# Keys and values of a bidirectional mLSTM and attention block as one product of quarters in seven products

## The chip, the cores and the metric

The kernel runs on one core of a Trainium2 chip. The metric is the device time of one execution in microseconds (us); 1239.61 us is the median of three runs of the kernel before (1238.98 to 1239.66). A core has a matrix engine (PE, which multiplies a stationary 128x128 tile by a moving tile of up to 512 columns into PSUM), a vector engine (DVE), an activation engine (ACT), GpSimd (POOL), and queues that issue transfers (DMAs): those of SP, ACT and POOL here.

## The reference

One layer over 1024 tokens of width 1024. Everything below is fp32 in the reference; the kernel splits each factor of a product into a high and a low part and takes three matmuls for each product.

```python
def rms(x, g):
    xf = x.astype(jnp.float32)
    return xf * lax.rsqrt(jnp.mean(xf * xf, axis=-1, keepdims=True) + EPS) * g.astype(jnp.float32)

# per layer:  p = rms(x, g1) @ w_in, its columns cut into
#   mLSTM:     q|k 0:1024 (behind a 5-wide convolution and silu), v 1024:1536, o 1536:2048, gates 2048:2064
#   attention: q 2064:2576, k 2576:3088, v 3088:3600
# x = x + concat(mlstm, attention) @ w_out ;  x = x + relu(rms(x, g2) @ w_1)**2 @ w_2

def diff_attention_group(qa, ka, va, q_g, k_g, ...):
    q = rms(q, q_g) * (HD_A ** -0.5)          # over 64 values of a head
    k = rms(k, k_g)
    logits = jnp.einsum('bmhqd,bmhkd->bmhqk', qblk, k) + bias
```

Two of these column blocks matter here: the attention keys (512 columns, called keys below) and the mLSTM values (512 columns, called values). The norm of a row of x, a factor `rcol` for each token, can be taken before or behind the product, since it scales rows.

## The kernel before

The activations stand transposed: `hhi[k]` and `hlo[k]` (k = 0 to 7, 128 channels by 1024 tokens) are the high and low part of x times the gain g1, not yet scaled by `rcol`. A weight tile is loaded raw, its high part made on ACT or DVE, and its low part by a subtraction on DVE or POOL.

The opening runs in this order on PE. [...] The values come first (L239): for each of 8 channel blocks, 8 token blocks and 3 matmuls, 192 matmuls of 512 columns into eight PSUM banks, as `x` arrives by SP. Then keys and gates together (`pkg`, L138 to L140 in the helper `mm3`): 8 token blocks with 48 matmuls each, of 256 or 272 columns. Then the queries (`pqa`): 192 matmuls of 512. Then the projections `pj_c` of the mLSTM queries and keys, in columns c4, c0 and so on, 48 matmuls of 512 each. From c0 on, a table of times places work between matmuls (six matmuls to a tick).

Beside the products, `head_norm` (L339 to L349) makes the norm of a token block's heads: a scaled copy from PSUM on ACT, a square on ACT, a sum and an addition on DVE, a power on POOL (L89), and a multiplication on DVE that is put off to the next block (`norm_end`). `gt` (L436) takes the gates out of the same PSUM tile. `head_turn` (L357) transposes normed heads on PE (tiles `pz`, two PSUM buffers of the tag sA) and splits the result on ACT and DVE into `zz`, which ACT's queue stores. `gates()` (from `pgt`, L446) turns the gates into decays: a chain of small steps over PE, DVE, ACT and POOL with tiles `pe`, `pm`, `pt`, also of sA. It runs during the queries. `distance_bias` fills a table of 2048 distances by 32 small DVE operations. POOL loads the row-wise x (`xr`, L251) for `rcol`.

Of the kernel before, what the change touches and what calls it, by code (L numbers as in the profile page):

```python
# [10 lines left out]
F32 = mybir.dt.float32  # L11
# [5 lines left out]
P = 128  # L17
S = 1024
# [29 lines left out]

@with_exitstack
def hybrid_block_kernel(ctx: ExitStack, tc: tile.TileContext, xT, xR, w_v, w_kg, w_c, w_va, w_qa, w_o, w_1, w_2, vec, rel, outT):  # L50
# [139 lines left out]
    stp = sctx.enter_context(tc.tile_pool(reuse_waits="tile", name="start", bufs=2, side="right"))  # L190
    with tc.tile_pool(reuse_waits="tile", name="ps0", bufs=8, space=PSUM) as ps0:
        lam = stp.tile([P, 256], F32, name="lam", bufs=1)
        total = stp.tile([P, NC], F32, name="total", bufs=1)
        rpad = stp.tile([P, 32], F32, name="rpad", bufs=1)
        rrow = stp.tile([P, 32], F32, name="rrow", bufs=1)
        pv = [ps0.tile([P, HB], F32, tag="pv", name=f"pv{t}") for t in range(NC)]

        for _ in range(9):
            nc.tensor.matmul(pv[0][:, 0:P], ones, ones, start=True, stop=True)
        xts = {}  # L200
        for k in range(KT):

            parts = 2 if k < 2 else 1
            n = S // parts
            xts[k] = xt = stp.tile([P, S], F32, tag="xt", name=f"xt{k}", bufs=4)
            if k == 0:

                whi, wlo, raw_v = w_tiles("v0")
                nc.scalar.dma_start(raw_v[:, 0:HB], w_v[0][:, 0:HB])

                nc.scalar.activation(mhalf, ones[:, 0:16], AF.Copy, scale=-0.5)
                nc.vector.tensor_copy(whi[:, 0:HB], raw_v[:, 0:HB])
            elif k % 2 == 0:
                whi, wlo, wload = wstage(f"v{k}", nc.vector)
                wload(w_v[k // 2], 0, 1024)
            for i in range(parts):
                sl = slice(i * n, (i + 1) * n)
                if k == 0 and i == 0:
                    nc.sync.dma_start(vecs[:, 0:V_CW], vec[:, 0:V_CW])
                load = nc.sync.dma_start(xt[:, sl], xT[k][:, sl])  # L220
                nc.scalar.activation(hhi[k][:, sl], xt[:, sl], AF.Copy, scale=vcol(V_G1 + k))
                last = nc.vector.scalar_tensor_tensor(
                    hlo[k][:, sl], xt[:, sl], vcol(V_G1 + k), hhi[k][:, sl].bitcast(F32), op0=ALU.mult, op1=ALU.subtract
                )
                if k == 0:

                    h = slice(i * HB, (i + 1) * HB)
                    if i == 1:
                        nc.sync.dma_start(raw_v[:, h], w_v[0][:, h])
                        nc.scalar.activation(whi[:, h], raw_v[:, h], AF.Copy)  # L230
                    nc.vector.tensor_tensor(wlo[:, h], raw_v[:, h], whi[:, h].bitcast(F32), op=ALU.subtract)
            o = (k % 2) * HB
            ops = [(hhi[k], whi), (hlo[k], whi), (hhi[k], wlo)]
            order = [(t, i) for t in range(NC) for i in range(3)]
            if k == 0:
                order = [(t, i) for h in range(2) for i in range(3) for t in range(4 * h, 4 * h + 4)]
            for t, i in order:
                a, b = ops[i]
                nc.tensor.matmul(  # L239
                    pv[t], a[:, t * P : (t + 1) * P], b[:, o : o + HB], start=k == 0 and i == 0, stop=k == KT - 1 and i == 2  # L240
                )
            if k == 2:
                with tc.issue_after(load.ins):
                    nc.sync.dma_start(vecs[:, V_CW:], vec[:, V_CW:V_LM])
                    nc.sync.dma_start(lam, vec[:, V_LM:])
            if k == 5:
                with tc.issue_after(last.ins):
                    parameters()
        for t in range(NC):
            xr = stp.tile([P, S], F32, tag="xt", name=f"xr{t}", bufs=4)  # L250
            nc.gpsimd.dma_start(xr, xR[t])  # L251
            nc.scalar.activation(xr, xr, AF.Square, accum_out=total[:, t : t + 1])
        nc.vector.tensor_scalar(rcol, total, 1.0 / D, EPS, op0=ALU.mult, op1=ALU.add)
        rsqrt(rcol, rcol, NC)
        nc.gpsimd.memset(rpad, 0.0)
        nc.vector.tensor_copy(rpad[:, 0:NC], rcol)
        nc.vector.transpose(rrow, rpad)
        for g in range(4):
            nc.gpsimd.dma_start(r_dram[:, 32 * g : 32 * g + 32], rrow[32 * g : 32 * g + NC, :])
        nc.gpsimd.dma_start(rb, bass.AP(tensor=r_dram.tensor, offset=r_dram.offset, ap=[[0, P], [1, S]]))  # L260
        vr = [stp.tile([P, S], F32, tag="xt", name=f"vr{i}", bufs=4) for i in range(4)]
        vr = [vr[t // 2][:, (t % 2) * HB : (t % 2 + 1) * HB] for t in range(NC)]
        for t in range(NC):
            if t % 2 == 0:
                nc.scalar.activation(vr[t], pv[t], AF.Copy, scale=rcol[:, t : t + 1])
            else:
                nc.vector.tensor_scalar(vr[t], pv[t], rcol[:, t : t + 1], None, op0=ALU.mult)
            nc.scalar.dma_start(vm_dram[t], vr[t])
# [67 lines left out]
    def head_norm(pool, src, z, t, name):  # L336

        zt = z
        nc.scalar.activation(zt.rearrange("p (a b) -> p a b", a=src.shape[1]), src, AF.Copy, scale=rcol[:, t : t + 1])  # L339
        sq = pool.tile([P, 8, 64], F32, tag="zsq", name=f"zsq{name}{t}", bufs=2)  # L340
        nc.scalar.activation(sq.rearrange("p a b -> p (a b)"), zt, AF.Square)
        ss = pool.tile([P, 8], F32, tag="zss", name=f"zss{name}{t}", bufs=2)
        nc.vector.tensor_reduce(ss, sq, axis=mybir.AxisListType.X, op=ALU.add)
        last = nc.vector.tensor_scalar(ss, ss, 64 * EPS, None, op0=ALU.add)
# [4 lines left out]
        ends.append(lambda: nc.vector.tensor_tensor(z8, z8, ss[:, :, None].to_broadcast([P, 8, 64]), op=ALU.mult))  # L349

# [6 lines left out]
    def head_turn(pool, tag, bufs, z, g, is_q):  # L357
# [7 lines left out]
        for h in range(NH):  # L365
# [16 lines left out]
            nc.scalar.dma_start(dst[h][g], zz.bitcast(F32))  # L382
# [4 lines left out]
    def distance_bias():  # L387

        rt = kgp.tile([NH, 32], F32, name="rt")
        nc.sync.dma_start(rt, rel.rearrange("b h -> h b"))  # L390
        bt = kgp.tile([NH, 2048], F32, name="bt")
        nc.vector.memset(bt[:, 2047:2048], 0.0)
        for b, first, end in _buckets():
            nc.vector.tensor_scalar(
                bt[:, first:end], rt[:, b : b + 1].to_broadcast([NH, end - first]), -1.0, None, op0=ALU.mult
            )
        nc.scalar.dma_start(bt_dram, bt)

    def key_weights(i):

        w = w_tiles(f"kg{i}", 1088)
        raw = w[2][:, 0 : 2 * N_HALF].rearrange("p (i n) -> p i n", i=2)
        hi, lo = (x.rearrange("p (i n) -> p i n", i=2)[:, :, 544 - N_HALF :] for x in w[:2])
        nc.sync.dma_start(raw, w_kg[i].rearrange("p (i n) -> p i n", i=2))
        nc.scalar.activation(hi, raw, AF.Copy)
        nc.vector.tensor_tensor(lo, raw, hi.bitcast(F32), op=ALU.subtract)
        return hi, lo

    wkg = [key_weights(i) for i in range(4)]
    halves = (slice(0, 256), slice(256, N_HALF))  # L410
    gt = gp.tile([P, 2, 8, NC], F32, name="gt")
    z1 = gp.tile([P, 4, HB], F32, name="z1")
    zs = [kgp.tile([P, 4, HB], F32, tag="z", name=f"z{i}", bufs=2) for i in range(2)]
    pkg = {}
    for t in range(NC):
        if t < NC - 1:

            ts = (t,) if t < NC - 2 else (t, t + 1)
            for a in ts:
                pkg[a] = psA.tile([P, 2, HB], F32, tag="pj", name=f"pkg{a}")  # L420

            blocks = [(k, t) for k in range(KT)] if len(ts) == 1 else sorted(
                ((k, a) for k in range(KT) for a in ts), key=lambda x: (x[0] + 1.5 * (x[1] - t), x[1])
            )
            for n, (k, a, j) in enumerate((k, a, j) for k, a in blocks for j in range(2)):
                tt = slice(a * P, (a + 1) * P)
                hi, lo = wkg[k // 2]
                mm3(
# [1490 lines left out]
```

## Time and profile before

| what | number |
|---|---|
| median of three runs | 1239.61 us (1238.98 to 1239.66) |
| the profiled execution's own time | 1239.08 us |
| its span | 1236.9 us |
| granted clock of PE | full in all of the 40 slices |
| PE busy | 1228.3 us, 99% of the span |
| DVE, ACT, POOL busy | 817.0, 621.7, 240.7 us |

The profiled execution has 2.2 us around its span. A page of the profile gives busy times, a chain of waits (followed back from the last instruction to what released it) and groups of equal instructions. Since PE is nearly never idle, the place to look is how many matmuls there are, how long one takes when the next follows at once (its pitch; the duration shown for one is longer, because matmuls overlap), and where PE waits at all.

### The profile page before, as it was taken

To read this page: it belongs to the slowest core of one execution; us is meant where nothing else is said; L and a number is where in the kernel's file an instruction comes from. 1 tells how busy PE (TensorE), PEld (TensorE's weight loads), DVE (VectorE), ACT (ScalarE), POOL (GpSimd) and SP (SyncE) were. 2 spreads that over 40 slices of the span, in tenths; PEclk is the share of its full clock that TensorE was granted. 3 is DMA by queue.
4 is the path that set the end of the run, shared out by engine and by line. 5 is a ranking of instruction groups with operands and counts; after the bars stand their busy time and mean duration, and the time that the engine had idled before them with its cause. 6 is when DMAs were issued, how large, how long until landed. Compare 5 with 4: busy or idle time off the path is not lost.

```text
span 1236.9 us, 17075 instructions
## 1 busy us (share of the span) xinstructions
PE 1228.3 (99%) x6397; PEld 1029.4 (83%) x6397; DVE 817.0 (66%) x1154; ACT 621.7 (50%) x1070; POOL 240.7 (19%) x268
## 2 busy tenths in 40 slices
PE   9999999999999999999999999999999999999998
PEld 8998788888878878888887888888888888888887
DVE  6335668895267796774789886766655765468654
ACT  7334437777356676664465454454544433333332
POOL 1133513473334363321000000000000000014001
PEclk9999999999999999999999999999999999999999
DMA  9514262364364585526545773534459655445732
GB/s 346 207 41 165 45 226 81 113 157 123 124 223 160 167 287 162 177 92 234 184 145 166 244 247 136 170 130 157 148 212 343 245 165 193 147 132 163 221 111 94
DMA packets 102750, 212.77 MB, mean 172 GB/s; under 512 B 9096, under 2 KB 21896, under 8 KB 102664
## 3 DMA queue, kind: packets, MB, share of 16 engines
q1 hardware_dynamic: 78164, 154.11, 38.8%
q10 hardware_dynamic: 15272, 31.89, 6.7%
q0 software_dynamic: 9232, 25.70, 6.3%
q8 instruction: 50, 0.82, 0.3%
q14 instruction: 32, 0.26, 0.1%
HBM read 153.36 MB, written 58.30 MB: 171 GB/s over the span
## 4 chain that ended last, share of the span: by engine, by line
PE 90%; DVE 4%; DMA 2%; ACT 1%; issue 1%; POOL 1%; ACTq 0%; SPq 0%; DVEq 0%; POOLq 0%
PE z L1746 8%; PE z L1745 8%; PE z L1744 8%; PE m L1415 7%; PE m L1417 7%; PE m L1416 7%; PE pav L1018 4%; PE pva L889 4%; PE pv L239 4%; PE pl L978 4%; PE pw L138 3%; PE pw L140 2%; PE pw L139 2%; PE pj_c L138 2%; PE pj_c L140 2%; PE pj_c L139 2%
## 5 line engine op out<-in xcount | busy, mean ns | idle before, releaser
L1789 POOL TENSOR_TENSOR zx<-zx,res 128x512 f32<-128x512 f32 x4 | 8.7, 2181 | 492.0 <-DVE zx L1787 492.0
L1746 PE MATMUL z<-wbh,wa0l 128*128 128x512 f32 x224 | 87.4, 390 | 0.1
L983 DVE CUSTOM_DVE_ANT_0 l<-pl,toe 128x1024 f32<-128x1024 f32 x64 | 76.3, 1221 | 16.6 <-PE pl L978 15.9
L1744 PE MATMUL z<-wbh,wa0h 128*128 128x512 f32 x224 | 87.2, 389 | 0.0
L1745 PE MATMUL z<-wbl,wa0h 128*128 128x512 f32 x224 | 87.1, 389 | 0.0
L1745 PE MATMUL z<-wel,wa1h 128*128 128x512 f32 x224 | 87.1, 389 | 0.0
L1744 PE MATMUL z<-weh,wa1h 128*128 128x512 f32 x224 | 87.1, 389 | 0.0
L1746 PE MATMUL z<-weh,wa1l 128*128 128x512 f32 x224 | 87.1, 389 | 0.0
L1328 ACT ACTIVATE wbh<-g 128x1024 fp32r<-128x1024 f32 x28 | 29.7, 1061 | 90.2 <-PE z L1746 53.0
L1328 ACT ACTIVATE weh<-g 128x1024 fp32r<-128x1024 f32 x28 | 29.7, 1061 | 90.2 <-PE z L1746 53.4
L989 ACT ACTIVATE l<-l,sm 128x1024 f32<-128x1024 f32 x64 | 73.2, 1149 | 0.5 <-DVE sm L983 0.5
L1331 DVE TENSOR_TENSOR wel<-g,weh 128x1024 fp32r<-128x1024 f32 x28 | 35.2, 1257 | 56.6 <-ACT weh L1328 56.6
L1464 ACT ACTIVATE sq<-sq 128x512 f32<-128x512 f32 x48 | 30.2, 630 | 82.5 <-DVE sq L1503 65.7
L1331 DVE TENSOR_TENSOR wbl<-g,wbh 128x1024 fp32r<-128x1024 f32 x28 | 35.4, 1265 | 53.5 <-ACT wbh L1328 53.3
L1018 PEld LDWEIGHTS pav<-v,at 128*128 128x128 f32 x512 | 61.5, 191 | 3.4 <-issue 1.1
L1018 PE MATMUL pav<-v,at 128*128 128x128 f32 x512 | 62.7, 275 | 0.0
L978 PE MATMUL pl<-kk,q 64*128 64x512 f32 x384 | 55.3, 410 | 0.9 <-DVE sm L983 0.9
L138 PE MATMUL pj_c<-hhi,w_c 128*128 128x512 f32 x128 | 53.1, 414 | 0.0
L138 PE MATMUL pw<-mix,hi_wo 128*128 128x512 f32 x128 | 52.0, 406 | 0.0
L140 PE MATMUL pj_c<-hhi,w_c 128*128 128x512 f32 x128 | 50.3, 393 | 0.0
L139 PE MATMUL pj_c<-hlo,w_c 128*128 128x512 f32 x128 | 50.1, 391 | 0.0
L140 PE MATMUL pw<-mix,lo_wo 128*128 128x512 f32 x128 | 50.0, 391 | 0.0
(450 smaller groups left out, 3575.1 us busy)
## 6 DMA issues: line engine op xcount, KB each, us to landing
g<-g_dram SPq DMA_DIRECT2D x56, 512.0 KB, 3.9
g_dram<-gs SPq DMA_DIRECT2D x64, 256.0 KB, 4.4
g_dram<-sq ACTq DMA_DIRECT2D x42, 256.0 KB, 2.2
kk<-k_dram POOLq DMA_DIRECT2D x16, 512.0 KB, 6.0
raw_wo<-in_w_o_dram SPq DMA_DIRECT2D x16, 512.0 KB, 4.9
re<-in_w_dram SPq DMA_DIRECT2D x16, 512.0 KB, 4.4
ro<-in_w_dram SPq DMA_DIRECT2D x16, 512.0 KB, 3.8
zt<-in_w_dram SPq DMA_DIRECT2D x16, 512.0 KB, 3.9
```

The costliest lines, as they stand in the source:

```text
L138: nc.tensor.matmul(out, ahi, bhi, start=start, stop=False)
L139: nc.tensor.matmul(out, ahi, blo, start=False, stop=False)
L140: latest[0] = nc.tensor.matmul(out, alo, bhi, start=False, stop=stop).ins
L978: nc.tensor.matmul(it.pl[x][:, sl], hd.q[r, i, qi * P : (qi + 1) * P], hd.kk[r, j, sl], start=n == 0, stop=n == 2)
L983: nc.vector.tensor_tensor_reduce(lt, it.pl[m], hd.toe[:, off : off + S], 1.0, 3.0e38, ALU.add, ALU.min, it.sm[:, m : m + 1])
L1018: nc.tensor.matmul(it.pav[:, 0:P], at, it.head.v[:, c], start=c == 0, stop=c == NC - 1)
L1415: nc.tensor.matmul(p, wh, xh, start=go, stop=False, skip_group_check=True)
L1416: nc.tensor.matmul(p, wh, xl, start=False, stop=False, skip_group_check=True)
L1417: nc.tensor.matmul(p, wl, xh, start=False, stop=stop and k == 3, skip_group_check=True)
L1744: nc.tensor.matmul(p, wh, gh, start=go, stop=False, skip_group_check=True)
L1745: nc.tensor.matmul(p, wh, gl, start=False, stop=False, skip_group_check=True)
L1746: nc.tensor.matmul(p, wl, gh, start=False, stop=end, skip_group_check=True)
```

## The change

Keys and values are now one product. Write x times g1 as quarters of channels by tokens, A11 and A12 for the first 512 tokens (channels 0 to 511 and 512 to 1023), A21 and A22 for the last 512; and the weights of keys and of values as upper and lower halves, w_k and w_v. A product of quarters takes 4 channel blocks by 4 token blocks by 3 matmuls, 48 matmuls of 512 columns. Eight of them would give keys and values of all tokens; the change uses seven, with sums of quarters (Winograd's form), in this order: K0, K1 (which give the keys of the first 512 tokens), T1, T2, T3, V1, T4. They are added up in two sets of four PSUM banks, X (K0, T2, T3, T4) and Z (K1, then T1 and V1), and ACT and DVE take each interim sum out of a bank.

The sums of weights are made by transfers that add in place, issued by POOL (`add_in`): w_v to minus w_k, then minus w_v's lower half, then w_v, then w_k's lower half. The sums of activations are DVE and ACT instructions. Some sources are loaded a second time (`load_v1`, `load_x21`).

The gates now share 528 columns with the queries (`pqa`, 48 matmuls of 256 or 272 for a token block) instead of the keys. Keys leave PSUM unscaled; `key_norm` takes their norm beside that of the queries, so that in the first four token blocks of the queries POOL makes two powers. `distance_bias` runs on ACT in four portions in those blocks. `gates()` begins after the last query block, with the transposes `pgt`; its other steps stand in the table of the c0 columns. Stores of `zz` and of the values go by SP. From the third c column on the order of instructions is the old one.

The order of the opening is no longer written out: a class `Plan` holds jobs with what they read and write, an engine and a cost, and emits them by a list schedule with latest times, worked backwards from a PE that takes 0.682 us for three matmuls from 4.9 us on.

```diff
+class Plan:
+    def job(self, how, reads, writes, due=None):
+        self.jobs.append([how, reads, writes, due])
+    def run(self):
...
+        lag = {"PE": 0.3, "ACT": 0.12, "DVE": 0.12, "NO": 0.0, "SP": 0.6, "POOL": 0.6}
...
+            if "PE" in how:
+                at[i] = 4.9 + 0.682 * k
...
-            order = [(t, i) for t in range(NC) for i in range(3)]
...
-                nc.tensor.matmul(
-                    pv[t], a[:, t * P : (t + 1) * P], b[:, o : o + HB], start=k == 0 and i == 0, stop=k == KT - 1 and i == 2
-                )
...
+        def add_in(reads, writes, dst, x, kb=512):
+            job({"POOL": (kb, lambda: nc.gpsimd.dma_start(dst(), x(), accum_op=add))}, reads + writes, writes)
...
+        turn = [(i // 4, i % 4) for i in range(8)] + [(2 + m % 2, m // 2) for m in range(8)]
+        def product(to, a, an, name, slots, start, stop):
+            for j, t in turn:
...
+                    for n, (x, y) in enumerate(((ah, bh), (ah, bl), (al, bh))):
+                        latest[0] = nc.tensor.matmul(
+                            o, x[:, tt], y, start=start and j == 0 and n == 0, stop=stop and j == 3 and n == 2,
...
+        product("X", A11, "A", "k0", K0, True, False)
...
+        product("Z", A12, "B", "k1", K1, True, True)
...
+            scaled(kr[j], kr[j], -1.0, [f"kr{j}"], [f"kr{j}"])
+            add_in([], [f"kr{j}"], lambda j=j: kr[j], lambda j=j: src(w_v, j), 256)
...
+        product("Z", SB, "S", "t1", T1, True, False)
...
+            add_in(n, k, lambda i=i: kt[i][:, 0:S], lambda i=i: flat(v1[i]))
+            add_in([], n, lambda i=i: flat(v1[i]), lambda i=i: w_v[i])
...
+            add_in([], [f"kr{2 * i}", f"kr{2 * i + 1}"], lambda i=i: kt[i][:, 0:S], lambda i=i: w_k[2 + i])
+        product("X", A21, "C", "t2", T2, False, False)
...
+        product("X", SB, "S", "t3", T3, False, False)
...
+        product("Z", A21, "C", "v1", V1, False, True)
...
+        product("X", A22, "D", "t4", T4, False, True)
...
-            xr = stp.tile([P, S], F32, tag="xt", name=f"xr{t}", bufs=4)
-            nc.gpsimd.dma_start(xr, xR[t])
...
+            nc.sync.dma_start(flat(xr[t]), xR[t])
...
-            nc.scalar.dma_start(dst[h][g], zz.bitcast(F32))
+            nc.sync.dma_start(dst[h][g], zz.bitcast(F32))
...
+    def key_norm(t):
+        zt = zs[t // 4][:, t % 4]
...
+        rsqrt(ss, ss, 8)
...
+        def end():
+            nc.vector.tensor_scalar(ss, ss, rcol[:, t : t + 1], None, op0=ALU.mult)
+            nc.vector.tensor_tensor(z8, z8, ss[:, :, None].to_broadcast([P, 8, 64]), op=ALU.mult)
...
+        if t < 4:
+            key_norm(4 + t)
...
+        if t in (2, 3, 4, 5):
+            distance_bias(t - 2, out.ins)
...
-    row_block(w_qa, "qa", nc.vector, qa_done)
-    norm_end()
+    gate_steps = gates()
+    next(gate_steps)
     pj0 = proj(w_c[4], "c4")
...
+    for n in range(9):
+        heapq.heappush(table, (0.3 + 1.2 * n, 10**6 + n, next, (gate_steps, None)))
```

The order of instructions shows what the planner made of it at three places. First POOL's queue in the opening (`raw_k` are the tiles kr and kt of the weight sums, `xtv` those of w_v's lower half). Before, two of the eight loads of `xr` shown:

```order
L255 MEMSET rpad 128x32
L492 MEMSET er_1420 1x72
L251 DMA xr_529<-in_xR_dram 128x1024
L251 DMA xr_532<-in_xR_dram 128x1024
L89 TENSOR_TENSOR rcol<-rcol,mhalf 128x8
```

And now:

```order
L321 DMA raw_k_269<-in_w_v_dram 128x512 x2
L321 DMA raw_k_270<-in_w_v_dram 128x512 x2
L321 DMA raw_k_269<-xtv_261 128x1024
L321 DMA raw_k_270<-xtv_262 128x1024
L321 DMA xtv_261<-in_w_v_dram 128x1024
L321 DMA raw_k_269<-in_w_k_dram 128x1024
L321 DMA xtv_262<-in_w_v_dram 128x1024
L321 DMA raw_k_270<-in_w_k_dram 128x1024
```

Eight plain loads have become ten adding transfers, and each of the later ones waits for an earlier one of the same tile or for its readers.

Second, DVE in the second query block. Before, it was a block of keys (numbers tell the blocks apart):

```order
L436 TENSOR_SCALAR gt<-pkg_882,rcol 128x16
L343 TENSOR_REDUCE zssk_935<-zsqk_933 128x8
L344 TENSOR_SCALAR zssk_935<-zssk_935 128x8
L349 TENSOR_TENSOR z_613<-z_613,zssk_877 128x512
L436 TENSOR_SCALAR gt<-pkg_940,rcol 128x16
```

And now:

```order
L761 TENSOR_TENSOR z_920<-z_920,zssk_1054 128x512
L752 TENSOR_REDUCE zssk_1130<-zsqk_1128 128x8
L753 TENSOR_SCALAR zssk_1130<-zssk_1130 128x8
L688 TENSOR_TENSOR z_971<-z_971,zssq_1064 128x512
L899 TENSOR_SCALAR gt<-pqa_1070,rcol 128x16
L721 TENSOR_TENSOR zzFalse_1124<-pzFalse_1119,zzFalse_1124 128x512
L682 TENSOR_REDUCE zssq_1139<-zsqq_1137 128x8
L683 TENSOR_SCALAR zssq_1139<-zssq_1139 128x8
L760 TENSOR_SCALAR zssk_1130<-zssk_1130,rcol 128x8
```

A block's `gt`, and the low part `zzFalse` of the transposed keys, stand behind two multiplications that each wait for a power of POOL, where one did.

Third, PE at the end of the queries. Before, `pgt` came in the middle of the queries:

```order
L139 MATMUL pqa_1245<-w_qa_1168,hhi_202 128x512
L140 MATMUL pqa_1245<-w_qa_1168,hlo_210 128x512
L446 MATMUL pgt<-ident,gt 64x128 x2
L138 MATMUL pqa_1356<-w_qa_1153,hhi_195 128x512
L139 MATMUL pqa_1356<-w_qa_1153,hhi_195 128x512
```

And now, with numbers left out of no name but `pgt`:

```order
L217 MATMUL pqa_1457<-w_qa_910,hlo_210 128x272
L708 MATMUL pzFalse_1572<-ident,z_920 128x128 x4
L768 MATMUL pgt<-ident,gt 64x128 x2
L215 MATMUL pj_c_1624<-hhi_195,w_c_1620 128x512
L216 MATMUL pj_c_1624<-hlo_203,w_c_1620 128x512
```

The gate transposes stand directly behind the last matmul of the queries, whose gates they read, and all of c4 stands behind them.

More of the change, by code (lines that the diff above doesn't have):

```diff
@@ L49, in hybrid_block_kernel @@
 @with_exitstack
-def hybrid_block_kernel(ctx: ExitStack, tc: tile.TileContext, xT, xR, w_v, w_kg, w_c, w_va, w_qa, w_o, w_1, w_2, vec, rel, outT):
+def hybrid_block_kernel(ctx: ExitStack, tc: tile.TileContext, xT, xR, w_v, w_k, w_c, w_va, w_qg, w_o, w_1, w_2, vec, rel, outT):
     nc = tc.nc
@@ L269, in hybrid_block_kernel @@
+    for n, t in enumerate((4, 5, 6, 7, 0, 1, 2, 3)):
+        if n % 2 == 0:
+            nc.scalar.activation(vr[t], vr[t], AF.Copy, scale=rcol[:, t : t + 1])
+        else:
+            nc.vector.tensor_scalar(vr[t], vr[t], rcol[:, t : t + 1], None, op0=ALU.mult)
+        nc.sync.dma_start(vm_dram[t], vr[t])
     sctx.close()
@@ L385, in head_turn @@
                 yield
[L387 to L428, printed above, removed]
-                    pkg[a][:, j, 0 : halves[j].stop - halves[j].start], hhi[k][:, tt], hlo[k][:, tt],
-                    hi[:, k % 2, halves[j]], lo[:, k % 2, halves[j]], k == 0, k == KT - 1,
-                )
-                if n % 8 == 7:
-                    step()
-        p = pkg[t]
-        g = p[:, 1, 256:272].rearrange("p (i r) -> p i r", i=2)
-        nc.vector.tensor_scalar(gt[:, :, :, t], g, rcol[:, t : t + 1], None, op0=ALU.mult)
-        head_norm(kgp, p[:, :, 0:256], zs[t // 4][:, t % 4], t, "k")
-        if t == 2:
-            distance_bias()
-        if t == 4:
-            pending.append(head_turn(kgp, "zz", 4, zs[0], 0, False))
@@ new lines, in distance_bias @@
+    def distance_bias(n, last):
+        if n == 0:
+            rt = kgp2.tile([NH, 32], F32, name="rt")
+            nc.sync.dma_start(rt, rel.rearrange("b h -> h b"))
+            bt = kgp2.tile([NH, 2048], F32, name="bt")
+            nc.gpsimd.memset(bt[:, 2047:2048], 0.0)
+            table_of[:] = rt, bt
+        rt, bt = table_of
+        with tc.issue_after(last):
+            for b, first, end in list(_buckets())[n::4]:
+                nc.scalar.activation(
+                    bt[:, first:end], rt[:, b : b + 1].to_broadcast([NH, end - first]), AF.Copy, scale=-1.0
+                )
+        if n == 3:
+            nc.gpsimd.dma_start(bt_dram, bt)
@@ new lines, in hybrid_block_kernel @@
+    table_of = []
+    def key_norm(t):
+        zt = zs[t // 4][:, t % 4]
+        sq = kgp.tile([P, 8, 64], F32, tag="zsq", name=f"zsqk{t}", bufs=2)
+        nc.scalar.activation(sq.rearrange("p a b -> p (a b)"), zt, AF.Square, scale=rcol[:, t : t + 1])
+        ss = kgp.tile([P, 8], F32, tag="zss", name=f"zssk{t}", bufs=2)
+        nc.vector.tensor_reduce(ss, sq, axis=mybir.AxisListType.X, op=ALU.add)
+        last = nc.vector.tensor_scalar(ss, ss, 64 * EPS, None, op0=ALU.add)
+        rsqrt(ss, ss, 8)
+        with tc.issue_after(last.ins):
+            norm_end()
+        z8 = zt.rearrange("p (a b) -> p a b", b=64)
+        def end():
+            nc.vector.tensor_scalar(ss, ss, rcol[:, t : t + 1], None, op0=ALU.mult)
+            nc.vector.tensor_tensor(z8, z8, ss[:, :, None].to_broadcast([P, 8, 64]), op=ALU.mult)
+        ends.append(end)
@@ L556, in row_block @@
                 )
[L557 removed]
+                if n % 8 == 7:
                     step()
[L559 to L571 removed]
@@ L577, in hybrid_block_kernel @@
     drain()
+    zz2ctx.close()
     kgctx.close()
```

451 lines of the change are left out of this document (358 added, 93 removed).

## The prediction

> **What bounds the kernel now.** First the page's busy times and clock row:
>
> ```profile
> PE 1228.3 (99%) x6397; PEld 1029.4 (83%) x6397; DVE 817.0 (66%) x1154; ACT 621.7 (50%) x1070; POOL 240.7 (19%) x268
> PEclk9999999999999999999999999999999999999999
> ```
>
> PE is idle for 1236.9 − 1228.3 = 8.6 us in all, and its granted clock is full throughout. Next, what PE waited for up to 260 us, past the whole stretch that the change touches:
>
> ```profile
> PE pv L199 <- POOL ones L76: 1.1, 1, 1.1
> PE pzTrue L368 <- DVE zzTrue L376: 0.5, 1, 0.5
> PE pd L744 <- ACT kt L128: 0.4, 1, 0.4
> PE pv L239 <- ACT hhi L221: 0.2, 1, 0.2
> ```
>
> Only 2.2 us, of which 0.5 lies in the projections c4. So in this stretch the time is the number of matmuls times their pitch. The chain of waits gives the pitch, and the ends of the stages:
>
> ```profile
> 1.16 3.14 DMA xt<-in_xT_dram
> 4.39 0.73 ACT hhi L221
> 5.17 43.84 PE pv L239 x192
> 83.81 0.44 PE pzFalse L368 x4
> 97.19 0.23 PE pqa L138
> ```
>
> The value product starts at 5.17 and its 192 matmuls of 512 columns take 43.84, so 0.2283 each. Keys with gates run from 5.17 + 43.84 = 49.01 to 97.19, with four groups of transposes of 0.44: 48.18 − 1.76 = 46.42 for 384 matmuls of 256 or 272 columns, 0.1209 each.
>
> **What the change removes.** Before, values and queries are 192 + 192 matmuls of 512. Now seven products of 48 make 336, and the 384 short ones remain, with queries in place of keys. So 384 − 336 = 48 matmuls of 512 go: 48 × 0.2283 = **10.96 us**. Behind c0 the order on every engine is the old one, so what can take it back lies before that. If PE never waits, the products start at: K0 5.2, K1 16.1, T1 27.1, T2 38.0, T3 49.0, V1 60.0, T4 70.9, and the queries at 81.9.
>
> **The start.** The first products need the same 256 KB of x and 256 KB of weights, and each engine's first conversions:
>
> ```profile
> L221 ACT ACTIVATE hhi<-xt,vecs 128x512 fp32r<-128x512 f32 x4 | 2.8, 724 | 2.6 <-DMA xt<-in_xT_dram 2.6
> L222 DVE SCALAR_TENSOR_TENSOR hlo<-xt,vecs,hhi 128x512 fp32r<-128x512 f32 x4 | 2.9, 751 | 1.4 <-ACT hhi L221 1.4
> L231 DVE TENSOR_TENSOR w_v<-raw_v,w_v 128x512 fp32r<-128x512 f32 x2 | 1.4, 687 | 0.0
> ```
>
> Before, four token blocks came ahead of the first matmul on `hlo`; now the third matmul needs it. `hhi` ends at 4.39 + 0.73 = 5.12, `hlo` at 5.9, and PE wants it at 5.63: 0.3 late. The first load of x now stands ahead of the small vector load on SP (0.38), which is worth up to as much. I take 0; the bounds are −0.4 and +0.3.
>
> **DVE and ACT in the opening.** The sums, the interim results out of PSUM and the conversions fall on these two. Up to the first norm DVE's order holds, by count, 32 scalar_tensor_tensor (0.751), 56 tensor_tensor (0.687), 8 tensor_scalar (0.752 at most, that of the row below), 4 casts and 4 subtractions on 1056 columns:
>
> ```profile
> L267 DVE TENSOR_SCALAR vr<-pv,rcol 128x512 f32<-128x512 f32 x4 | 3.0, 751 | 3.4 <-PE pv L239 3.4
> L406 DVE TENSOR_TENSOR w_kg<-raw_kg,w_kg 128x1056 fp32r<-128x1056 f32 x4 | 4.9, 1247 | 5.0 <-ACT w_kg L405 5.0
> L212 DVE CAST w_v<-raw_v 128x512 fp32r<-128x512 f32 x1 | 0.4, 427 | 2.6 <-DMA raw_v<-in_w_v_dram 2.6
> 85.34 0.69 DVE L381 TENSOR_TENSOR zzFalse<-pzFalse,zzFalse 128x512 fp32r<-128x512 f32 x1 [1.24 <-ACT zzFalse L128]
> 85.94 0.68 DVE L343 TENSOR_REDUCE zssk<-zsqk 128x8 f32<-128x512 f32 x1
> ```
>
> That is 24.0 + 38.5 + 6.0 + 1.7 + 5.0 = 75.2 us by durations. The last two rows start 0.60 apart at 0.69 long, so an operation that follows at once costs some 0.09 less; over 104 that leaves 66. There are 81.9 − 4.4 = 77.5 us for it. ACT holds 20 `hhi` of 0.724, some 56 copies of about 0.65, 8 squares of 1.24 and three of 1.08: near 64 us. DVE fits by its pitch with 11 us over and by full durations with 2. Nothing before shows DVE this full in a stretch, so a wait at a single hand-over of banks is uncertain: 0 where it keeps pace; and where every operation takes its full duration and DVE idles again for the 1.4 ahead of `hlo` and the 3.4 ahead of `vr` that the rows show, 75.2 + 4.8 − 77.5 = 2.5 us. I take 0, by the pitch row, since DVE's queue is seldom empty here.
>
> **The adding transfers.** Ten go through POOL. No row shows an adding transfer, nor one from SBUF to SBUF; the nearest are POOL's loads of 512 KB in the busiest part of the opening:
>
> ```profile
> 20.00:30.00 10.00, 10.00 (x45) 8.28 (x45) 6.43 (x14) 7.63 (x11) 2.63 (x5) 1.00 0.93 347
> DMA to landing us min/median/max: 3.7/6.0/8.1
> ```
>
> The second row is of the tile `xr`, whose eight loads these are. The need: the sum in `raw_k` is read for T1 until about 28; then minus w_v's lower half is added, which T2 needs split by 38.0 less 0.63 and 0.69 for the two conversions, 36.6. So a transfer may take 8.6 us. Behind it the `xtv` sum is made, wanted for T3 by 49.0 − 1.4 = 47.6: two in a row may take 19.6, or 9.8 each. The last ones, from T2's start to T4's, have 30. At 6.0 all are hidden, and the worst seen, 8.1, still is. I take 0. Above 8.6 it grows, to (2L − 19.6) for a landing of L.
>
> **The query stage.** Per token block a chain runs: `gt`, copy, square, sum, power, multiplication, and now, in four of eight blocks, a key norm's sum, power and multiplication as well:
>
> ```profile
> L436 DVE TENSOR_SCALAR gt<-pkg,rcol 128x16 f32<-128x16 f32 x7 | 1.8, 251 | 13.9 <-PE pkg L140 13.8
> L339 ACT ACTIVATE z<-pkg,rcol 128x512 f32<-128x512 f32 x7 | 4.8, 689 | 25.0 <-DVE gt L436 25.0
> L341 ACT ACTIVATE zsqk<-z 128x512 f32<-128x512 f32 x6 | 3.8, 632 | 0.2
> L343 DVE TENSOR_REDUCE zssk<-zsqk 128x8 f32<-128x512 f32 x6 | 4.1, 685 | 7.1 <-ACT zsqk L341 7.1
> L89 POOL TENSOR_TENSOR zssk<-zssk,mhalf 128x8 f32<-128x8 f32 x6 | 11.5, 1910 | 28.8 <-DVE zssk L344 28.8
> L349 DVE TENSOR_TENSOR z<-z,zssk 128x512 f32<-128x512 f32 x5 | 3.4, 685 | 0.0
> ```
>
> With one power this is 0.25 + 0.69 + 0.63 + 0.69 + 1.91 + 0.69 = 4.85, under a block's 48 × 0.1209 = 5.80. With the key's power ahead on POOL it is 6.76, 0.96 over. The copy waits for its block's `gt`, and `gt` stands on DVE behind the multiplications that wait for those powers; so a block that overruns makes the next copy late, and PE, two PSUM tiles ahead, waits for the tile. The third transposes of keys wait too, for the low part of the first, which stands behind the same two multiplications. Bounds: 0, where the key's power is always done early, and 4 × 0.96 = 3.8. Walking the order with these durations gives 0.3 at the third block, 1.1 at the third transposes and 0.3 later: **+1.7**.
>
> **The gates and c4.** `pgt` now reads the last block's gates directly behind its last matmul: a wait for `gt`, 0.25 and a hand-over. Behind it come the query transposes, whose multiplications wait for the last two powers. Before, that chain cost 0.5:
>
> ```profile
> 146.42 0.60 DVE zssq L343
> 147.37 1.50 POOL zssq L89
> 149.28 1.64 POOL zssq L89
> 151.56 0.76 DVE zzTrue L376
> 152.37 0.66 PE pzTrue L368 x4
> L174 POOL TENSOR_TENSOR w_c<-raw_c,w_c 128x1024 fp32r<-128x1024 f32 x3 | 7.2, 2395 | 0.0
> ```
>
> Now a low part of w_c (2.395) stands on POOL ahead of those powers, and the key transposes that used to be over take banks in c4. I count 0.3 for `pgt` and 0.5 at each of two query transposes, 1.3 less the old 0.5: **+0.8**; bounds −0.5 and 2.4 less 0.5, +1.9.
>
> In c0 the gate chain's small steps now stand between projections. Its longest part is ACT's:
>
> ```profile
> L521 ACT ACT_TABLE_LOAD x1 | 1.3, 1283 | 0.0
> L539 DVE COPY ucol<-pt 128x64 f32<-128x64 f32 x1 | 0.2, 223 | 3.4 <-PE pt L538 3.4
> ```
>
> ACT swaps tables for it between the silu of c4 and that of c0, so `pt` may come late by up to a load and its neighbours, 1.6; the convolution of c0 that stands behind the three copies of `pt` on DVE has 11 us of the next projection as cover. **+0.2**, bounds 0 and 1.6. The bias table on ACT (32 small operations, ahead of nothing that PE needs at once) I take as nothing; if not, it is in the bounds of the query stage.
>
> **The sum**, against the profiled execution's 1239.08: −10.96 + 0 + 0 + 0 + 1.7 + 0.8 + 0.2 = −8.26, so 1230.8; the median stands 0.5 above that execution, which makes **1231.3**.
>
> **Rivals.** *All hand-overs hidden*: for it, PE waited for 0.5 us in this stretch before, on the same chains; against, two powers in a block. Then −10.96 − 0.5 on 1239.61: 1228.2. Chance 0.17. *DVE is the bound of the opening*: for it, 75 us of work in 77.5; against, the overlap of neighbours. The 2.5 us from above: 1233.8, and with the query stage at its upper bound as well (2.1 more) 1235.9. Chance 0.19. *The adding transfers are slow*: their sums read two operands and write one, in place, so L may be twice the median load, or 13 to 16 us instead of 6; T3 then starts 2 × 13 − 19.6 = 6 to 12 us late. The gain of 8.3 is gone at L = 14; at 16 the time is 1243.7, slower than before. Against it, 347 GB/s is moved beside such loads and the ten sums have 4 × 256 KB + 6 × 512 KB, 4.2 MB, in some 40 us. Chance 0.07. *POOL's port*: issues of POOL may be held up while DVE works. The rows of `xr` show none:
>
> ```profile
> L251 POOL DMA_DIRECT2D xr<-in_xR_dram x8 | 4.5, 562 | 24.9 <-DVE hlo L222 18.6 <-ACT xr L252 3.3 <-DMA raw_kg<-in_w_kg_dram 2.5
> ```
>
> 0.56 each, in a stretch where DVE is busy 64% of the time. Were they held for that share, each would take 0.56 / 0.36 = 1.6, 1.0 more; at the worst landing, 8.1, T2 would start 9.1 − 8.6 = 0.5 late, 1231.8. Chance 0.05. [...] *The change moves work but PE runs no faster* (waits of 8 us spread over all seven products): 1239, chance 0.03.
>
> **How the numbers follow.** The forecast has 0.49. A difference of 0.2%, 2.5 us, is what this kernel can tell from none; the three runs before lie within 0.7. Faster by more than that: forecast, hidden, DVE and port, 0.49 + 0.17 + 0.19 + 0.05 = **0.90**. Same: the change that brings nothing and the slow transfers that land between 12 and 15 us, 0.03 + 0.02 = **0.05**. Slower: the rest of the slow transfers, **0.05**. The range reaches from hidden with half the gain at the start, **1228.0**, to DVE with most of the query stage's upper bound, **1235.3**; left out are the slow transfers, the change that brings nothing and the worst of DVE.
>
> **What would show it.** Right: a product group of 336 matmuls from 5.2 to about 82 at 0.228; in the list of waits up to 250 us some 1 us at the key transposes and at `pgt` and the query transposes each; the adding transfers land in 6 to 8 us. Wrong: waits of PE in the opening on low parts made from `raw_k` or `xtv` (transfers late) or on copies out of the banks X and Z (DVE or ACT late); a pitch over 0.23; or waits at c0 over 1 us.

## The result, and the profile after

The changed kernel takes **1250.7 us** (median of four, 1249.44 to 1251.16) against 1239.63 for the kernel before in the same runs: a ratio of 1.0088, 95% interval 1.0071 to 1.0106. It is slower by 11 us, where 8 us faster was forecast; the 48 matmuls are gone, and 22 us came back. The changed kernel's page gives these busy times and clock:

```profile
PE 1224.3 (98%) x6349; PEld 1024.4 (82%) x6349; DVE 851.5 (68%) x1206; ACT 648.1 (52%) x1154; POOL 243.7 (20%) x272
PEclk9999998999999999999999999999999999999999
```

PE has the 48 matmuls fewer (6397 to 6349), but stands still for 1248.7 − 1224.3 = 24.4 us instead of 8.6, and its clock falls below full in one of the 40 slices. What PE waited for in the whole execution, the longest five of the list:

```profile
PE pj_c L217 <- POOL w_c L960: 5.9, 1, 5.9
PE pav L1357 <- ACT at L1349: 3.9, 1, 3.9
PE pvz L416 <- DVE z L455: 2.9, 1, 2.9
PE pl L1317 <- DVE sm L1322: 1.2, 2, 0.7
PE pv L313 <- POOL ones L153: 1.1, 1, 1.1
```

The first three are new. They lie at 31, 201 and 376 us: one in the opening, one in the c columns of the mLSTM, and one in attention, whose code the change does not touch. The stages can be laid side by side by the first and last start of their matmuls. The kernel before:

```profile
L138 PE MATMUL pj_c<-hhi,w_c x128: 387/393/500, 144.4 to 267.1; 128*128 128x512 f32 x128
L889 PE MATMUL pva<-w_va,hhi x128: 387/393/496, 268.6 to 335.1; 128*128 128x512 f32 x128
L1415 PE MATMUL m<-x6h,wbh x64: 387/389/497, 652.9 to 913.4; 128*128 128x512 f32 x64
L1744 PE MATMUL z<-wbh,wa0h x224: 389/389/397, 927.7 to 1226.8; 128*128 128x512 f32 x112
```

The changed kernel:

```profile
L215 PE MATMUL pqa<-w_qa,hhi x128: 276/283/388, 87.7 to 138.0; 128*128 128x256 f32 x64, 128*128 128x272 f32 x64
L215 PE MATMUL pj_c<-hhi,w_c x128: 387/397/775, 139.1 to 272.3; 128*128 128x512 f32 x128
L1228 PE MATMUL pva<-w_va,hhi x128: 387/393/496, 273.8 to 340.3; 128*128 128x512 f32 x128
L1754 PE MATMUL m<-x6h,wbh x64: 387/389/507, 664.3 to 924.5; 128*128 128x512 f32 x64
L2083 PE MATMUL z<-wbh,wa0h x224: 389/389/397, 938.8 to 1237.9; 128*128 128x512 f32 x112
```

| stretch | before | after | what it lost |
|---|---|---|---|
| start to the queries | | 87.7 | 5.8 against the 81.9 that PE needs |
| queries to c4 | | 51.4 | 1.9 against 384 × 0.1209 + 7 × 0.44 = 49.5 |
| c columns (`pj_c` to `pva`) | 124.2 | 134.7 | 10.5, of which 2.0 are gate and key transposes that moved in (144.4 − 10.96 − 81.9 − 49.5) |
| `pva` to the MLP (`m`) | 384.3 | 390.5 | 6.2 |
| MLP (`m` to last `z`) | 573.9 | 573.6 | nothing |

**The opening.** DVE's timeline of the changed kernel around the first wait, and its windows of 4 us (PE, PEld, DVE, ACT, POOL busy, granted clock, DMA share, GB/s):

```profile
28.48 0.43 DVE L367 TENSOR_SCALAR xtv<-xtv 128x512 f32<-128x512 f32 x1 [4.79 <-DMA xtv<-in_w_v_dram]
28.83 0.75 DVE L362 SCALAR_TENSOR_TENSOR hs<-xtxb,vecs,hs 128x512 f32<-128x512 f32 x1
30.09 0.69 DVE L455 TENSOR_TENSOR z<-pvz,z 128x512 f32<-128x512 f32 x1
24.00:28.00 4.00, 4.00 (x18) 3.00 (x16) 0.00 (x0) 1.25 (x2) 0.00 (x0) 1.00 1.04 254
28.00:32.00 4.00, 1.09 (x4) 0.48 (x3) 3.52 (x7) 3.52 (x7) 0.00 (x0) 0.98 0.04 9
32.00:36.00 4.00, 4.00 (x12) 3.03 (x12) 4.00 (x7) 2.69 (x5) 1.00 (x2) 0.59 0.48 92
```

DVE, which was to be the busiest engine of the opening, idled for 4.79 us before the negation of `xtv`, which is read first by the sums for T2, in transfers issued at 32.87 and 35.87; behind it in the queue stood what T1 was waiting for. The DMA engines were full (1.04) at only 254 GB/s. And the wait was paid twice: in the 4 us after it the granted clock was 0.59. Of the 5.8 us, 0.9 were lost ahead of this: K1 starts at 17.0, for the 16.1 of an unbroken start.

**The queries.** PE's two waits in this stage, 0.6 and 0.5, lie at 100 and 101 us. DVE's row ahead of them, and POOL's row of the same time:

```profile
97.07 2.43 DVE L753 TENSOR_SCALAR zssk<-zssk 128x8 f32<-128x8 f32 x1
97.06 2.41 POOL L251 TENSOR_TENSOR w_c<-raw_c,w_c 128x1024 fp32r<-128x1024 f32 x1
```

An addition on 128x8 values, 0.17 us in the blocks before it, took 2.43 and ended with POOL's subtraction on a weight of the c columns. The multiplication of the keys that PE waited for stands right behind it. The two rows coincide in the other profiles of this stage too (94.55 and 92.85 in two runs below); that the one holds the other up was not tested.

**The c columns.** SP's timeline, then POOL's:

```profile
170.64 0.38 SPq L1034 DMA_DIRECT2D qs<-sc_dram  x1
176.67 0.33 SPq L864 DMA_DIRECT2D decb<-dec_dram  x1
177.08 2.12 SPq L1034 DMA_DIRECT2D e<-m_dram  x1
179.77 2.25 SPq L722 DMA_DIRECT2D q_dram<-zzTrue  x1
182.06 1.43 SPq L952 DMA_DIRECT2D raw_c<-in_w_c_dram  x1
191.31 0.37 SPq L1034 DMA_DIRECT2D e<-m_dram  x1
196.31 2.21 POOL L1048 TENSOR_SCALAR_AFFINE_SELECT e<-e 128x512 f32<-128x512 f32 x2 [7.47 <-DMA e<-m_dram]
198.53 2.34 POOL L960 TENSOR_TENSOR w_c<-raw_c,w_c 128x1024 fp32r<-128x1024 f32 x1
```

POOL makes the low part of the next weight column (198.53) only behind its selection on `e`, which waits for the second load of `e` (191.31). That load stood in SP's queue behind the load of `decb`, held until the decays had been written to memory (176.67), and then waited for the store of the last query tile (179.77) to land, because `e` takes the tile that this store reads. In the kernel before, c4 started 5.3 us later than here, and the second load of `e` was issued sooner:

```profile
182.29 0.36 SPq L697 DMA_DIRECT2D e<-m_dram  x1
```

Against its stage it is 14 us later now.

**Attention.** ACT's row, PE's row behind it, and the window that follows:

```profile
371.84 1.06 ACT L205 ACTIVATE w_o<-raw_o 128x1024 fp32r<-128x1024 f32 x1 [8.52 <-PE po L217]
375.70 2.98 PE L1357 MATMUL pav<-v,at 128*128 128x128 f32 x16 [3.89 <-ACT at L1349]
376.00:380.00 4.00, 4.00 (x24) 3.98 (x22) 4.00 (x7) 3.03 (x6) 1.36 (x2) 0.58 0.32 83
```

ACT stood 8.52 us before the high part of an output-gate weight, until PE's last matmul of the column then running (`po`). Its source had been issued at 358.21 and had landed in 3.9; what was missing was the tile to write to. The exponentials of attention stood behind it.

### The profile page after: what moved, and what is told of

It is laid out like the page before. It is cut to its first block, busy times and chain, and to the rows that moved or that the text cites. A ratio compares the mean times of both kernels' runs of the same rounds, so it can differ in the third digit from the quotient of the medians.

```text
span 1248.7 us, 17181 instructions
## 1 busy us (share of the span) xinstructions
PE 1224.3 (98%) x6349; PEld 1024.4 (82%) x6349; DVE 851.5 (68%) x1206; ACT 648.1 (52%) x1154; POOL 243.7 (20%) x272
## 4 chain that ended last, share of the span: by engine, by line
PE 83%; DVE 5%; DMA 5%; issue 2%; ACT 2%; POOL 2%; SPq 0%; ACTq 0%; DVEq 0%; POOLq 0%
PE z L2085 8%; PE z L2084 8%; PE z L2083 8%; PE m L1754 7%; PE m L1755 7%; PE m L1756 7%; PE pav L1357 4%; PE pva L1228 4%; PE pl L1317 3%; PE pw L215 3%; PE pw L217 2%; PE pw L216 2%; PE pa L1345 2%; PE pv L416 2%; PE pvz L416 1%
```

## Experiments

Each is the changed kernel with the edit shown, unless said otherwise. Medians are of four runs or more; the kernel before stood at 1239.3 to 1239.5 beside them.

**The order of the opening.** Two ideas: DVE's queue is in the wrong order, or the transfers are too slow. First the order:

```diff
-            scaled(n1[j], n1[j], -1.0, [f"n{j}"], [f"n{j}"])
+            scaled(n1[j], n1[j], -1.0, [f"n{j}", "z03"], [f"n{j}"])
```

> In the planner the negation of w_v's lower half is made to follow the interim sums of the keys, so that DVE and ACT no longer stand before it while its load is under way (it landed at 28.46, issued 16.77). Theory D, that the order of DVE's queue is at fault (the work that T1 needs, behind an operation that T3 needs): the 2.9 us wait at T1 and the lower clock behind it (48 matmuls in 13.05 us rather than 10.96) go: 1245 to 1247 us. Rival B, that the transfers as a whole are the bound up to 28 us: T1's own operands come as late, the wait stays within 1 us of what it was: 1249.5 to 1251 us.

Measured 1247.9 (1247.33 to 1248.74), 2.8 less: between the two. The waits at T1 fell from 2.9 to 1.1, and DVE's longest idle time showed what stood behind the order:

```profile
25.98 0.75 DVE L362 SCALAR_TENSOR_TENSOR hs<-xtxb,vecs,hs 128x512 f32<-128x512 f32 x1 [3.27 <-DMA xtxb<-in_xT_dram]
```

Now T1's own operand, the last quarter of x, was late. So both hold: the order cost a part (2.8 us by the medians; in the profiles the queries start at 86.6 for 87.7), the transfers the rest. Second, the adding itself, in a kernel that leaves the sums of weights out:

```diff
-            job({"POOL": (kb, lambda: nc.gpsimd.dma_start(dst(), x(), accum_op=add))}, reads + writes, writes)
+            job({"POOL": (kb, lambda: nc.gpsimd.dma_start(dst(), x()))}, reads + writes, writes)
```

> The ten transfers of POOL copy instead of adding: same bytes, same queue, same order; the sums of weights are left out, so keys and values are not the reference's. Theory A, that an adding transfer takes about twice the DMA engines' time for a byte (in the changed kernel up to 90 us POOL's queue took 25.4% of them for 4.20 MB, SP's 58.6% for 18.32 MB) and that this makes the loads of the opening late: the last load of w_v's lower half lands near 25 rather than 28.5, the wait of 2.9 us at T1 is under 0.5, the queries start at 83 to 84.5 rather than 87.7: 1246 to 1247.5 us. Rival, that it is the bytes and not the adding: the landing moves by under 1 us and the time is 1249.5 to 1251.

Measured 1248.25 (1247.04 to 1249.58), 2.5 less, again between. Up to 80 us POOL's queue holds nothing but these ten transfers. In the changed kernel it took:

```profile
q0 software_dynamic: 1440, 4.19, 28.5%
```

and without adding, with DVE's row of the negation behind it:

```profile
q0 software_dynamic: 1184, 4.19, 15.1%
27.10 0.43 DVE L367 TENSOR_SCALAR xtv<-xtv 128x512 f32<-128x512 f32 x1 [4.02 <-DMA xtv<-in_w_v_dram]
```

The columns of a queue are packets, MB and share of the 16 engines. The same transfers took 15.1% as copies and 28.5% as sums, 1.9 times, as the first theory had it. (Up to 90 us, as in the expectation, a load of another tile falls into the queue of the run that copies.) But `xtv` came only 1.4 us sooner (27.10 for 28.48). Most of the delay is bytes: by 28 us the opening asks for all of x (4 MB), the keys' weights (2 MB), w_v's lower half (1 MB) and the first four sums (1 MB). The wait at T1, three of at most 1.5 us here, no longer drew a lower clock (1.00 from 27 to 36 us).

**SP's queue in the c columns.** Either the stores that went from ACT's queue to SP's are at fault (theory Q), or the gate chain that moved into c0 (rival G). First the stores back:

```diff
-            nc.sync.dma_start(dst[h][g], zz.bitcast(F32))
+            (nc.scalar if bufs == 2 else nc.sync).dma_start(dst[h][g], zz.bitcast(F32))
```

> The stores of the last four split query tiles (they use the tags qs and e) go by ACT's queue again, as before the change; all else as in the changed kernel (1250.7 us). Theory Q, that these stores stand in SP's queue ahead of the second load of e, which waits for the last store to land (issued 179.77, e at 191.31), so that POOL's selection and the low part of the next weight column are late and PE waits 5.9 us: the second e load is issued by about 183, the 5.9 us wait is gone and with it about 2 us at a lower clock: 1242 to 1244 us. Rival G, that the gate chain that moved into c0 is what makes e late, through the load of decb that holds SP from 170.6 to 176.7: the wait shrinks by 2 us at most, 1248 to 1250 us.

Measured 1247.35 (1246.59 to 1248.45), between the two forecasts. The second load of `e` was issued at 182.41, as Q said, yet PE still waited 3.5 us: the first load of `e` landed 10.7 us after its issue, and the second after 9.6. Then `decb`:

```diff
-        nc.sync.dma_start(decb, bass.AP(
+        nc.gpsimd.dma_start(decb, bass.AP(
```

> The load of decb, which waits for a round trip of the decays through memory, goes by POOL's queue instead of SP's; stores of the query tiles stay on SP. Theory Q: the first load of e and the store are issued some 3 to 4 us earlier at most, since the store waits for its tile (ready at about 175.4) and e for the store's landing; the wait of 5.9 us shrinks by 4 to 5: 1245 to 1247 us. Rival G: the hold of SP for 6 us is the cause, the wait is gone whole: 1242 to 1244 us, and POOL's low part is not later.

Measured 1245.93 (1244.44 to 1247.24); the time is in Q's range, but the wait fell to 3.7 only, half of what Q said. Both together (the two edits above):

> Both edits at once: the last four query tiles are stored by ACT's queue and decb is loaded by POOL's. Alone they left 3.5 and 3.7 us of the 5.9. If SP's queue (the store and the hold together) is the whole cause, the second load of e is issued by about 178 and the wait is gone: 1242.5 to 1244.5 us. If the loads of e themselves are slow here (10 us each against 5.2 before) because the decays come out of the gates so late that e, qs, decb and a weight column all load at once, 1.5 to 3 us of the wait stay: 1245 to 1246.5.

Measured 1248.18 (1246.86 to 1249.1): over both forecasts, and not under either edit alone. Executions of one of these three kernels lie up to 2.8 us apart, so the profiles tell more: the c columns took 132.8, 132.1 and, with both, 131.2 us for 134.7, and two waits of 4.0 us together remained. So SP's queue isn't the whole cause. Then the gate chain's own pace:

```diff
-        heapq.heappush(table, (0.3 + 1.2 * n, 10**6 + n, next, (gate_steps, None)))
+        heapq.heappush(table, (0.3 + 0.6 * n, 10**6 + n, next, (gate_steps, None)))
```

> The nine steps of the gate chain stand in the table of the c0 columns at 0.3 + 0.6 n instead of 0.3 + 1.2 n, so the last of them comes 4.8 us sooner in the order; stores and loads stay on SP. If the chain's own place in c0 is what makes the decays late, m_dram, decb and e come 3 to 4.5 us sooner and the 5.9 us wait falls to 1.5 to 3: 1246 to 1248 us. If SP's queue alone is at fault, e stays where the store puts it, and the wait is 5 to 6: 1250 to 1251; PE may then wait for the gate steps itself.

Measured 1245.14 (1244.28 to 1245.84), with stores and `decb` still on SP. The wait for POOL's low part is gone whole, where the forecast left 1.5 to 3 us of it; a small one at a gate step took its place:

```profile
PE pav L1357 <- ACT at L1349: 3.9, 1, 3.9
PE pvz L416 <- DVE z L455: 3.1, 1, 3.1
PE pm L836 <- DVE mprow L829: 1.4, 1, 1.4
```

Both forecasts for this run missed on the good side: the c columns fell from 134.7 to 129.5 us (139.0 to 268.5). Rival G had the larger share: the pace alone takes 5.2 us off the c columns, both edits of SP's queue together 3.5. The queue still costs here, since the second load of `e` waits for the store as before (issued at 187.66).

**The turn of the weight slots.** Weight tiles take their slot by a count, modulo five while the mLSTM runs and modulo two after it. The change sets the count to 3 ahead of c4, which takes the free fourth slot for c4, where the old kernel had counted to 12. Both have the same number of calls behind that, so in the modulo of two they have opposite parity.

```diff
     wpools.pop()
+    wturn[0] += 1
```

> One count is added to the turn of the weight tiles where the number of slots goes from five to two, so that the two slots are taken in the turn that the kernel before had. Theory T, that the setting of that count by the change makes the third output-gate weight of the mLSTM take the slot which the current column still reads, so that ACT stands still from 363.3 to 371.8 and PE waits 3.9 us for the attention weights: that wait is gone, and with it the 2 us that the next columns lose: 1244 to 1246.5 us. Rival: ACT is late there because the attention's loads are late behind everything else; then the wait stays and the time is 1250 to 1251.

Measured 1244.68 (1242.02 to 1246.18): 6.0 less, as the theory had it, and the wait of 3.9 is gone from the list; ACT's high part of `w_o` runs at 360.92 with nothing ahead of it. The reverse, the same line in the kernel *before*:

> The kernel before with one count added to the turn of the weight slots where their number goes from five to two, so that it has the turn of the changed kernel, and nothing else. If the turn is the whole cause of the loss in attention, PE waits some 3.9 us for the attention weights here too and the time is 1244 to 1246 us; if it needs the changed kernel's other delays, 1239 to 1240.

Measured 1244.79 (1244.52 to 1245.17), 5.4 slower than the kernel before without it (ratio 1.0043, 1.0026 to 1.006). Its rows are those of the changed kernel to the hundredth:

```profile
367.10 1.06 ACT L128 ACTIVATE w_o<-raw_o 128x1024 fp32r<-128x1024 f32 x1 [8.52 <-PE po L140]
PE pav L1019 <- ACT at L1011: 3.9, 1, 3.9
```

One count, by itself, is worth 5.4 to 6 us; nothing else of the change has a part in it.

**Together.** All mends but the pace, and with the loads of w_v's lower half behind those of x (an artificial dependency in the planner):

```diff
-            load([], [f"n{2 * i}", f"n{2 * i + 1}"], dma(flat(v1[i]), w_v[2 + i]), 512)
+            load(["r3", "t3", "k13"], [f"n{2 * i}", f"n{2 * i + 1}"], dma(flat(v1[i]), w_v[2 + i]), 512)
```

> All mends at once: negation later in the planner's order, the two loads of w_v's lower half behind the loads of x, stores of the last query tiles on ACT's queue, decb on POOL's, the turn of the weight slots as before. By the sum of the parts (the opening 3 to 4, the c columns 5 to 8, attention 6) 1233 to 1237 us, which would beat the kernel before (1239.4). If the opening is bound by its bytes, or the loads of e stay slow, 1237 to 1241.

Measured 1238.04 (1235.94 to 1241.5; ratio 0.9989, 0.998 to 0.9999): as its second forecast had it, level with the kernel before; 4.2 us at POOL's low part are left, as after the two queue edits. Then the pace in place of those edits:

> Three mends: the opening (negation and loads of w_v's lower half later), the turn of the weight slots, and the gate steps at 0.3 + 0.6 n; stores and decb stay on SP. The run with all mends but this pace (1238.0 us) still waited 4.2 us for POOL's low part in the c columns; with the pace alone that wait was gone. If the pace alone settles the c columns: 1238.0 less 3 to 4, 1233.5 to 1235.5 us, with 1 to 1.5 us of wait at pm. If the wait comes back because the columns start 4 us sooner than with the pace alone, so that the gates have less time, 1236 to 1239.

Measured 1236.15 (1235.3 to 1238.68), at the edge of the second forecast, though no wait at POOL's low part is left in its list and 1.4 at `pm` is. And the stores on ACT's queue with it:

> As the run with the three mends, and the last query tiles stored by ACT's queue. If the pace alone settles it, the same within 1 us, 1233 to 1236 us; if SP's queue still matters once the gates are sooner, 1 to 2 us less than that run.

Measured 1234.36 (1233.82 to 1234.54): 1.8 less, so the stores in SP's queue do matter once the gates are sooner. At last the pace between:

> As the run before it, with the gate steps at 0.3 + 0.8 n: the last step 1.6 us later. The wait of PE at pm (1.4 us at 0.6 n) should be gone, and e still be in time: 0.5 to 1.5 us under that run, 1232 to 1235 us. If e comes late again, 1 to 3 us over it.

Measured **1234.2** (1233.46 to 1235.97), no different from the run before it, where 0.5 to 1.5 less was expected. The wait at `pm` fell from 1.4 to 0.3 and 0.9 at `pt` has come. Against the kernel before the ratio is 0.9959 (0.9943 to 0.9975): this version beats both. What PE waits for in it, the five longest:

```profile
PE pv L313 <- POOL ones L153: 1.1, 1, 1.1
PE pt L861 <- ACT u L853: 0.9, 1, 0.9
PE pvz L416 <- DVE z L455: 0.9, 4, 0.3
PE pv L416 <- ACT hhi L334: 0.9, 1, 0.9
PE pl L1318 <- DVE sm L1323: 0.9, 2, 0.6
```

Its queries still start at 85.7 for 81.9. Of these 3.8 us, 0.9 are lost at the start, 1.9 at T1 and in it, where PE waits four times for DVE's interim sums, and 1.1 in V1. ACT's row ahead of T1 shows one reason:

```profile
25.58 0.63 ACT L334 ACTIVATE w_t<-raw_k 128x512 fp32r<-128x512 f32 x1 [2.72 <-DMA raw_k<-in_w_v_dram]
```

A sum of weights that T1 itself reads landed late, and DVE's work for T1 stands behind it. No edit here took this away.

## Why the prediction was wrong

- **Removed work: right.** 48 matmuls fewer, 0.2283 each. The version without the long waits keeps 5 of the 10.96 us; 3.8 go in the opening and 1.7 in the c columns (127.9 for 124.2, with the 2.0 that moved in).
- **"Behind c0 the order on every engine is the old one, so what can take it back lies before that": wrong, and the costliest step.** The order was the old one, but two things that an order doesn't show had moved: when the loads of `e` can start, and which slot a weight tile takes. They cost some 8.5 us in the c columns and 6.2 up to the MLP, two thirds of the 22.
- **The start, taken as 0 with 0.3 as bound: 0.9**, by the start of K1.
- **c0, taken as +0.2 with 1.6 as bound: measured about 8 us in the columns behind it.** The chain `pt` was followed to DVE and ACT only. The decays also go out to memory and come back, as `decb`, `qs` and `e`, through SP's queue, to POOL and the next weight column; the write of `dec_dram` alone, 64 values, took 7.3 us to land. Of the store that moved to SP's queue only the issue was thought of, not the load that waits for its tile.
- **The adding transfers, taken as 0 from the landing of plain loads: half right.** The sums land in 4.5 to 8.5 us by the medians, and T2 and T3 did not wait for them. But the step gave no time to the four sums that T1 itself reads, which landed after 7.0 to 9.3 us, the last at 29.1, when T1 was to have started at 27.1. And it looked at each transfer's latency and never summed the bytes: the plain loads share the DMA engines with the sums (up to 80 us SP's queue took 56.4% of them, POOL's 28.5%), and the last took 11.7 us. With the order of DVE's queue and the clock that is 4.8 of the opening's 5.8 us.
- **DVE as the bound of the opening, a rival at 0.19: not so in the changed kernel.** DVE idled at loads. Its queue order came from a planner that counts loads at 380 GB/s and sums at 200; from 20 to 28 us the trace shows 254 to 270. In the version that beats both, the four waits in T1 are waits for a DVE that is busy for all of the 4 us from 28 on, so a little of this rival is there.
- **The query stage and `pgt`, +1.7 and 0.3: measured 1.9**, but not for the reason given, so the agreement is luck. In the version that beats both, the stage takes 135.4 − 85.7 = 49.7, nearly its bare matmuls, with the same two powers in a block: these cost nothing. The two waits seen in the changed kernel, 0.6 and 0.5, stand behind the addition that took 2.43 us. In the version that beats both it takes as long, but 4.2 us sooner, and PE does not wait; why it is in time there was not tested (the run that copies starts its queries as early, at 85.5, and waits).
- **The waits at c4's transposes, 0.5 each: nearly right**, 0.3 and 0.5 for the 1.0 counted; a third, of 0.3, lies in c0.
- **The rival that ends slower named slow adding transfers with T3 late.** The sign came true by other mechanisms. The rival of POOL's port: the ten issues took 0.86 to 1.09 us for 0.56, beside a DVE that was busy for 17.1 of the 18 us in which they ran (14 to 20 and 32 to 44): less than the 1.6 that this rival had beside a DVE busy for 64%. As copies they took 0.53 to 0.75, so part of the longer issue comes with the adding.
- **A wait's price was taken as its length.** Each of the three long waits drew 2 to 3 us more, at a lower clock: 12.7 us of waits cost near 19.5. In the opening 47 matmuls took 12.62 instead of 10.73; in the c columns a wait of 5.9 made 8.5; in attention one of 3.9 made 6.2. With 0.9 of the start and 1.9 of the queries that is the 22.

## What to carry to other kernels

A comparison of orders shows neither tile slots nor what waits on memory: after a change of one stage, count on what the later stages inherit, above all a rotating slot count and loads whose tile is still being stored. Before loads are called hidden, add up the bytes that a stage needs by its start, sums in place at 1.9 times, and set them against the rate that the trace shows there. A queue that works in order, as DVE's and SP's did here (idle for 4.79 us at the negation and for 5.65 at `decb`), should hold nothing that is needed late ahead of what is needed soon, and a list schedule can do just that when its transfers land sooner in the plan than on the chip (380 GB/s there, 254 here).

## What the runs showed of the hardware

After each of the changed kernel's waits of 2.9, 3.9 and 5.9 us PE's granted clock fell to about half for some 4 us (0.59, 0.58 and, behind the wait of 5.9, these windows):

```profile
198.00:202.00 4.00, 1.07 (x3) 0.89 (x4) 1.16 (x2) 0.26 (x1) 2.87 (x3) 0.64 0.03 5
202.00:206.00 4.00, 4.00 (x14) 3.42 (x13) 1.60 (x5) 1.95 (x7) 0.00 (x0) 0.51 0.33 126
206.00:210.00 4.00, 4.00 (x22) 3.39 (x22) 3.89 (x5) 3.97 (x4) 2.07 (x1) 1.00 0.00 0
```

Behind the wait of 5.9, matmuls of 512 columns start 0.43 us apart, and 0.23 from 206 us on. Waits of up to 1.5 us, at T1 in the run that copies, drew none (1.00). In between, the length alone does not decide. The run with both edits of SP's queue has a wait of 2.4 us at T1, ahead of the first window here, and one of 2.75 us for POOL's low part, ahead of the second; the run with all mends but the pace has one of 2.73 us, ahead of the third:

```profile
32.00:36.00 4.00, 4.00 (x14) 3.20 (x13) 4.00 (x8) 2.53 (x5) 1.16 (x2) 0.67 0.52 100
200.00:204.00 4.00, 4.00 (x23) 3.36 (x22) 3.82 (x9) 2.82 (x8) 0.00 (x0) 1.00 0.40 131
196.00:200.00 4.00, 4.00 (x14) 3.48 (x15) 3.44 (x6) 1.60 (x6) 0.00 (x0) 0.61 0.40 131
```

The granted clock is 0.67, full and 0.61. So of the four waits of 2.4 to 2.9 us here three drew a lower clock and one did not; what tells the cases apart stays open. And the ten adding transfers into on-chip memory held the DMA engines 1.9 times as long as copies of the same bytes (28.5% of the 16 engines up to 80 us against 15.1%).
